# A mixture-of-experts stack: the four experts with the fewest tokens on raw float32 weights in two column halves, and expert weights in 8 KB rows

## The chip, the cores and the metric

The kernel runs on one core of one Trainium2 chip. The metric is the device time of one execution, in microseconds (us). Times that are compared come from repeated runs; the profile is one execution, taken by the hardware profiler. TensorE multiplies, VectorE (DVE) and ScalarE (ACT) do elementwise work, POOL is GpSimd, and SP issues the weight transfers.

## The reference, cut to what matters

An input of 256 tokens with 1024 features goes through two stacks of two layers. Layers of the first stack hold two kinds of attention and a feed-forward network; layers of the second hold a dilated attention beside an mLSTM. The first layer of the second stack has a dense feed-forward network, the second one eight experts, of which every token uses two:

```python
def swiglu(x, w13, w2):
    a, g = jnp.split(x @ w13, 2, axis=-1)
    return (jax.nn.silu(a) * g) @ w2

def moe_ffn(x, router_w, router_b, w13, w2):
    logits = (x @ router_w).astype(jnp.float32) + router_b.astype(jnp.float32)
    top_v, top_i = lax.top_k(logits, TOP_K)
    wts = jax.nn.softmax(top_v, axis=-1)
    gate = jnp.einsum('bsk,bske->bse', wts, jax.nn.one_hot(top_i, N_EXPERTS, dtype=jnp.float32)).astype(x.dtype)
    y = jnp.zeros_like(x)
    for e in range(N_EXPERTS):
        y = y + gate[..., e:e + 1] * swiglu(x, w13[e], w2[e])
    return y
```

An expert has a hidden width of 3584, so its three matrices are 11.01 million float32 numbers, 44.04 MB. With the inputs of the reference the router gives the experts 52, 36, 120, 63, 64, 53, 51 and 73 tokens.

## The kernel before

**Weights.** All weights stream from memory once, in the order of their use, in pieces of 1 MB (`Weights.add`, `Stream.load`, issued by SP at L200). Each piece goes to the next slot of a cycle (`_CYCLES`). For the experts the cycle has fourteen slots: four parts of the `wide` tile, four groups of four small tiles `s2` (four transfers of 256 KB each, 2 KB in a partition's row), four `raw` tiles, one pair of `bc` tiles (two transfers of 512 KB), and the tile `xTl`. A slot is loaded again as soon as its piece is used (`self.done`).

**Three passes.** `Stream.ahead` splits a piece, two blocks of 128 x 512 at a time: ScalarE copies it to `wh` in a shorter float format (L218), VectorE takes `wl` = raw - `wh` (L219). The input is split in the same way, and `mac` (L363) makes three matmuls of a block:

```python
        nc.tensor.matmul(out, xh, wh, start=first, stop=False)
        nc.tensor.matmul(out, xh, wl, start=False, stop=False)
        nc.tensor.matmul(out, xl, wh, start=False, stop=last)
```

They are L366, L367 and L368 in the rows. `wh` and `wl` have five tiles each, of two blocks.

**An expert** (`expert`, L1384) has room for 128 tokens. `gather` (L1351) picks its tokens by a one-hot matmul (L1366) and transposes them; 14 hidden blocks of 256 units take 8 weight blocks each, and after every 6, 4 and 4 of them (`_SEG`) the second matrix takes 4 blocks per hidden block: 168 blocks in 42 pieces. `hidden` multiplies the two halves and transposes the result by two matmuls; `scatter` puts the rows back (L1409, L1410). Experts go in the order 0 to 7. The gather of the next expert begins in the last segment. An expert with more than 128 tokens would send the kernel through a second pass over all of them, under `tc.If`.

**The order of the rest.** Nothing is scheduled by the compiler. Work beside the matmuls is written as generators; `tick`, called after every two weight blocks, advances each of them by one step, and `_WAIT` says how many ticks a generator lets pass at a named point (`wait("s2")`), so that its input is ready when its next TensorE instruction comes up. `softmax_quad` (L628) does four score matrices of an attention: after `wait("s2")` it transposes the probabilities (L665), after `wait("s3")` it multiplies them with the values (L673). `head_norm` (L591) normalises queries and keys, with VectorE's L602 after a reciprocal root on POOL (L443, L444), four ticks later. In `first_block` (L806) the projections run in the order: queries, keys, first attention, values and the rest. In `second_block` (L1146): the gate z of the mLSTM, its input, queries, keys, values, the attention beside the mLSTM, the branch gates (VectorE adds, ScalarE takes tanh), then `branches` with the mLSTM's branch M ahead of the attention's A.

## Time and profile before

| What | Value |
|---|---|
| Time, median of 3 runs | 2345.89 us (2345.5 to 2346.64) |
| The profiled execution | 2344.98 us, its span 2343.2 us |
| TensorE matmuls | 2269.1 us busy, 97% |
| VectorE | 1822.2 us busy, 78% |
| ScalarE | 1441.0 us busy, 61% |
| Weights by SP's queue | 566.44 MB, 66.5% of 16 DMA engines |
| Transfers of expert weights | 217 of 1 MB, 384 of 256 KB, 44 of 512 KB |

A busy share is a mean over the span, and the span has two kinds of stretch: the two stacks with their attention, up to some 1340 us, and the experts, from there to 2326 us. The 40 slices in the profile show them side by side: one digit is the busy share of a slice of 58.6 us in tenths. Matmuls overlap on TensorE, so one matmul's bar is longer than the beat at which they follow each other; the beat is read from the starts. One float32 matmul leaves two records in the trace. An instruction's bracket names how long its engine had been idle before it and whose work ended that.

### The profile page before, as it was taken

How to read it: one execution, taken by the hardware profiler on the slowest of the kernel's cores; microseconds unless marked ns; L12 is line 12 of the kernel's file. 1: busy time of each engine (PE TensorE's matmuls, PEld its weight loads, DVE VectorE, ACT ScalarE, POOL GpSimd, SP SyncE). 2: the span in 40 equal slices, each digit the busy share in tenths (PEclk: the TensorE clock that was granted, in tenths of full speed). 3: DMA queues.
4: the chain of work that ended last, by engine and by line, in shares of the span. 5: the costliest groups of instructions: out<-in, count | busy, mean ns of one | idle time of the engine just before them, and what ended most of it. 6: DMA issues, size and time to landing. Idle time of an engine off the chain costs nothing. (4 is left out here: it accounts for less than half of the span.)

```text
span 2343.2 us, 30976 instructions
## 1 busy us (share of the span) xinstructions
PE 2269.1 (97%) x11041; PEld 1859.9 (79%) x11041; DVE 1822.2 (78%) x2672; ACT 1441.0 (61%) x2166; POOL 100.3 (4%) x163
## 2 busy tenths in 40 slices
PE   6999999999999999999998899999999999999997
PEld 5778888778888977788886688888888888888775
DVE  5866556867565677655767799999999999999988
ACT  4555444555444554444454488888888888888775
POOL 4100001100010000000100000000000000000000
PEclk9999999999999999999999899999999999999998
DMA  6435555435565444554544799999999999999981
GB/s 238 159 138 180 182 186 204 167 126 180 180 233 205 154 136 168 197 198 164 184 168 141 300 362 371 354 370 349 371 349 370 349 373 341 376 339 376 332 334 47
DMA packets 128162, 583.06 MB, mean 249 GB/s; under 512 B 14592, under 2 KB 14880, under 8 KB 74624
## 3 DMA queue, kind: packets, MB, share of 16 engines
q1 hardware_dynamic: 124416, 566.44, 66.5%
q0 software_dynamic: 3584, 14.56, 1.9%
q8 instruction: 89, 1.46, 0.2%
q14 instruction: 73, 0.60, 0.1%
HBM read 579.90 MB, written 1.05 MB: 248 GB/s over the span
## 5 line engine op out<-in xcount | busy, mean ns | idle before, releaser
L219 DVE TENSOR_TENSOR wl<-raw,wh 128x1024 fp32r<-128x1024 f32 x594 | 711.7, 1229 | 147.8 <-ACT wh L218 145.1
L366 PE MATMUL mm<-wh,xTh 128*128 128x512 f32 (+1 forms) x1904 | 762.0, 400 | 6.7 <-DVE s L602 3.3
L367 PE MATMUL mm<-wl,xTh 128*128 128x512 f32 (+1 forms) x1904 | 742.5, 390 | 8.8 <-DVE wl L219 8.8
L218 ACT CAST wh<-raw 128x1024 fp32r<-128x1024 f32 x594 | 611.9, 1050 | 122.6 <-PE mm L368 110.0
L366 PEld LDWEIGHTS mm<-wh,xTh 128*128 128x128 f32 x1904 | 359.3, 189 | 82.6 <-issue 11.7
L367 PEld LDWEIGHTS mm<-wl,xTh 128*128 128x128 f32 x1904 | 359.8, 189 | 76.0 <-DVE wl L219 9.9
L368 PE MATMUL mm<-wh,xTl 128*128 128x512 f32 (+1 forms) x1008 | 392.4, 389 | 2.1 <-DVE xTl L455 1.9
L366 PE MATMUL mm<-wh,s 128*128 128x512 f32 x968 | 386.2, 399 | 0.0
L368 PE MATMUL mm<-wh,s 128*128 128x512 f32 x968 | 378.5, 391 | 0.2 <-DVE s L458 0.2
L367 PE MATMUL mm<-wl,s 128*128 128x512 f32 x968 | 378.0, 391 | 0.0
L368 PE MATMUL mm<-wh,xTh 128*128 128x512 f32 x896 | 349.7, 390 | 0.0
L219 DVE TENSOR_TENSOR wl<-s,wh 128x512 fp32r<-128x512 f32 x384 | 242.2, 690 | 14.1 <-ACT wh L218 10.8
L219 DVE TENSOR_TENSOR wl<-wide,wh 128x1024 fp32r<-128x1024 f32 x196 | 235.1, 1222 | 17.0 <-ACT wh L218 6.2
L218 ACT CAST wh<-s 128x512 fp32r<-128x512 f32 x384 | 217.4, 620 | 23.2 <-PE mm L368 21.7
L218 ACT CAST wh<-wide 128x1024 fp32r<-128x1024 f32 x196 | 204.1, 1055 | 36.4 <-PE mm L368 33.0
L368 PEld LDWEIGHTS mm<-wh,xTl 128*128 128x128 f32 x1008 | 190.9, 189 | 43.7 <-DVE xTl L455 4.3
L366 PEld LDWEIGHTS mm<-wh,s 128*128 128x128 f32 x968 | 182.5, 189 | 39.4 <-issue 2.5
L368 PEld LDWEIGHTS mm<-wh,s 128*128 128x128 f32 x968 | 182.1, 188 | 39.7 <-DVE s L458 0.8
L367 PEld LDWEIGHTS mm<-wl,s 128*128 128x128 f32 x968 | 182.6, 189 | 35.3
L368 PEld LDWEIGHTS mm<-wh,xTh 128*128 128x128 f32 x896 | 168.3, 188 | 36.0
L454 ACT CAST s<-ax 128x256 fp32r<-128x256 f32 x178 | 66.4, 373 | 163.5 <-PE ax L452 163.5
L455 DVE TENSOR_TENSOR s<-ax,s 128x256 fp32r<-128x256 f32 x178 | 75.1, 422 | 68.2 <-ACT s L454 68.2
(287 smaller groups left out, 1934.0 us busy)
## 6 DMA issues: line engine op xcount, KB each, us to landing
raw<-in_wpre SPq DMA_DIRECT2D x197, 1024.0 KB, 4.8
wide<-in_wexp SPq DMA_DIRECT2D x97, 1024.0 KB, 6.5
s<-in_wexp SPq DMA_DIRECT2D x384, 256.0 KB, 6.4
raw<-in_wexp SPq DMA_DIRECT2D x96, 1024.0 KB, 6.6
xTl<-in_wexp SPq DMA_DIRECT2D x24, 1024.0 KB, 6.9
bc<-in_wexp SPq DMA_DIRECT2D x44, 512.0 KB, 6.9
raw<-in_wpre SPq DMA_DIRECT2D x8, 512.0 KB, 3.5
wide<-in_bias_b POOLq DMA_DIRECT2D x2, 1536.0 KB, 9.6
```

The source lines that it names most:

```text
L218: nc.scalar.copy(h, raw)
L219: nc.vector.tensor_tensor(l, raw, h.bitcast(F32), op=ALU.subtract)
L366: nc.tensor.matmul(out, xh, wh, start=first, stop=False)
L367: nc.tensor.matmul(out, xh, wl, start=False, stop=False)
L368: nc.tensor.matmul(out, xl, wh, start=False, stop=last)
L454: nc.scalar.copy(hi, ps)
L455: nc.vector.tensor_tensor(lo, ps, hi.bitcast(F32), op=ALU.subtract)
```

## The change

There are three edits.

1. **Ranking.** The experts are worked in order of their token counts, the large and the small ones alternating (`_RANK`): places 0, 2, 4 and 6 take the four with the most tokens, places 1, 3, 5 and 7 the four with the fewest; expert 0 always stands first. `rest`, the tail of the router, computes the ranks, and SP reads the index of the expert from the tile `r_which` (`place`, a register load) for the address of each piece. The small places have room for 64 tokens, and the second pass runs if an expert has more than its room.
2. **Raw weights.** In the small places no weight is split. The moving operand is the raw float32 block where the transfer put it; the stationary one is the input, 128 x 64 float32. Even blocks write the partitions 0 to 63 of the result, odd ones 64 to 127 (`tile_position`), so that two blocks use the two halves of the array's columns. `hidden_few` adds the halves and transposes at once, by four float32 matmuls with the 128 x 64 constant `fold2`. A slot becomes free when its matmuls are issued (`gone`), not when it is split.
3. **Slots.** The cycle of the expert weights has nine slots, all of 1 MB with 8 KB in a partition's row: `wide` four times, `raw` four times, `xTl`.

With them come moves in the blocks ahead: the first layer of `first_block` projects the values before the queries, `head_norm` waits five ticks instead of four, `second_block` takes the values first and z after the attention has begun, its gates are generators of their own, and branch A comes ahead of M. The waits s2 and s3 go from 4 and 3 to 5 and 4, and stay at 4 and 3 (`s2x`, `s3x`) in the attention beside the mLSTM; `h2` is 2. The table `_WAIT` and the constants' declarations are left out here.

```diff
+_RANK = [0, 4, 1, 5, 2, 6, 3, 7]
+_SMALL = 64
+_ROOMS = [_SMALL if r > 3 else 128 for r in _RANK]
...
-_FIRST, _THEN = ["0", "1", "2", "3", "s2a"], ["raw"] * _BUFS["raw"] + ["bc", "xT"]
-_CYCLES = [_FIRST + ["s2b", "s2c", "s2d"] + _THEN]
...
+_CYCLES = [["0", "1", "2", "3"] + ["raw"] * _BUFS["raw"] + ["xT"]]
...
-    ("bias", 3072, 1), ("v129", 2064, 1), ("m_g", 512, 1), ("junk", 256, 1), ("early", 800, 1),
+    ("bias", 3072, 1), ("v129", 2064, 1), ("m_g", 512, 1), ("junk", 256, 1), ("early", 928, 1),
...
-        if a == "bc":
-            return [k.row(1024).rearrange("p (n w) -> p n w", w=w) for _ in range(2)], 1024 // w
...
-        if a[:2] == "s2":
-            return [k.s2(1, 512) for _ in range(n)], 1
...
-            if self.held and self.slots[self.loaded][0] in ("bc", "xT"):
+            if self.held and self.slots[self.loaded][0] == "xT":
...
-                e = self.e if e < 0 else e
+                e = self.e if e < 0 else k.place(e)
...
-            p, j, m = parts[self.split]
+            p, j, m, plain = parts[self.split]
...
+            if plain:
+                self.ready[self.split] = [tiles[(j + i) // per][:, (j + i) % per] for i in range(m)]
+                self.split += 1
+                continue
...
-                del self.raw[p]
-                self.done = p
-                self.load(0)
+                self.gone(p)
...
+    def gone(self, p):
...
+        del self.raw[p]
+        self.free.add(p)
+        while self.done + 1 in self.free:
+            self.done += 1
+        self.load(0)
...
+        p, _, _, plain = self.order.parts[self.over]
...
+        if plain and (self.over == len(self.order.parts) or self.order.parts[self.over][0] != p):
+            self.gone(p)
...
-        for _ in range(4):
+        for _ in range(5):
...
-        yield from self.wait("s2")
+        yield from self.wait("s2" if beside is None else "s2x")
...
-            self.evac(p, pt)
+            nc.scalar.copy(p, pt)
...
-        yield from self.wait("s3")
+        yield from self.wait("s3" if beside is None else "s3x")
...
+                    self.finish(*self.late)
...
-        self.project(xT, 8, W(0, 512), later(prep_q), outer=4)
-        if not self.dry:
+        values = lambda outer: self.project(xT, 8, W(1792, 512), keep_v, outer=outer)
+        if l == 0:
+            values(4)
+        if not self.dry and l == 0:
...
+        self.project(xT, 8, W(0, 512), later(prep_q), outer=4 if l else 0)
...
-        self.project(xT, 8, W(1792, 512), keep_v)
+        if l:
+            values(0)
...
-        self.project(xT, 8, [("w_in_2", (l,), 2048, 512)], tanh_z, outer=4)
+        def keep_v(t, ps):
+            va[t] = self.s2(512)
+            self.evac(va[t], ps)
...
+        qT, kT, va = {}, {}, {}
+        self.project(xT, 8, [("w_in_2", (l,), 1024, 512)], keep_v, outer=4)
...
-        qT, kT, va = {}, {}, {}
...
-        def keep_v(t, ps):
-            va[t] = self.s2(512)
-            self.evac(va[t], ps)
...
-        self.project(xT, 8, [("w_in_2", (l,), 1024, 512)], keep_v)
...
+        self.project(xT, 8, [("w_in_2", (l,), 2048, 512)], tanh_z)
...
-                def gate(t, ps):
-                    g = G[t][:, D * n + 512 * j : D * n + 512 * j + 512]
-                    V.tensor_tensor(g, ps, bg[:, 512 * j : 512 * j + 512], op=ALU.add)
+                def gate(t, ps, g, b):
+                    V.tensor_tensor(g, ps, b, op=ALU.add)
+                    yield
...
-                self.project(xT, 8, [("w_gate_2", (l,), D * n + 512 * j, 512)], gate)
...
+                at = D * n + 512 * j
+                self.project(
+                    xT, 8, [("w_gate_2", (l,), at, 512)],
+                    lambda t, ps: gates.append(self.go(gate(t, ps, G[t][:, at : at + 512], bg[:, 512 * j : 512 * j + 512]))),
+                )
...
-        self.branches(G, ((M, ym, "w_br_m_2", 1), (A, ya, "w_br_a_2", 0)), l)
+        self.late = gates
+        self.branches(G, ((A, ya, "w_br_a_2", 0), (M, ym, "w_br_m_2", 1)), l)
...
-            V.reduce_max(most, ps, axis=AX.X)
...
+            n, rank, over, most, at = self.tiny(8), self.tiny(8), self.tiny(8), self.tiny(1), self.tiny(8)
+            every = [128, 8, 8]
+            V.tensor_tensor(n, ps, self.c("tie8"), op=ALU.add)
+            more, place = self.s2(8, 8), self.s2(8, 8)
+            V.tensor_tensor(more, n[:, None, :].to_broadcast(every), n[:, :, None].to_broadcast(every), op=ALU.is_gt)
+            V.reduce_sum(rank, more, axis=AX.X)
+            V.tensor_scalar(self.rooms, rank, 3.5, _SMALL - 128.0, op0=ALU.is_gt, op1=ALU.mult)
+            V.tensor_scalar(self.rooms, self.rooms, 128.0, None, op0=ALU.add)
+            V.tensor_tensor(over, ps, self.rooms, op=ALU.subtract)
+            V.reduce_max(most, over, axis=AX.X)
...
+            yield
...
+                place, rank[:, None, :].to_broadcast(every), self.c("rank8")[:, :, None].to_broadcast(every), op=ALU.is_equal
...
+            V.tensor_tensor(more, place, self.c("index8")[:, None, :].to_broadcast(every), op=ALU.mult)
+            V.reduce_sum(at, more, axis=AX.X)
+            V.tensor_copy(self.which, at)
+            yield
...
+                V.tensor_tensor(got, place[:, None].to_broadcast(both), src[:, :, None, :].to_broadcast(both), op=ALU.mult)
+                V.reduce_sum(dst, got, axis=AX.X)
+                yield
...
+    def place(self, i):
...
+        if i not in self.places:
+            self.places[i] = self.nc.values_load(
+                self.which[0:1, i : i + 1], engines=(mybir.EngineType.SP,), min_val=0, max_val=NE - 1
...
+        return self.places[i]
...
-            V.tensor_scalar(oh[:, t], self.c("iota"), key[:, t], None, op0=ALU.is_equal)
+            V.tensor_scalar(oh[:, t], self.c("iota" if room == 128 else "iota2"), key[:, t], None, op0=ALU.is_equal)
...
+        both = self.tl(self.keep, "xTh", [128, 2, 8, 128], F32R if room == 128 else F32)
...
-            self.split_T(lambda i: rows[n][:, 128 * i : 128 * i + 128], 4, both[:, 0, z], both[:, 1, z])
...
+            if room == 128:
+                self.split_T(src, 4, both[:, 0, z], both[:, 1, z])
+            else:
+                self.to_T(src, 4, both[:, 0, z, 0:room])
...
+        many = room == 128
...
+        def product(out, a, b, k, i, n):
...
+            if many:
+                self.mac(out, (a[:, 0, k], a[:, 1, k]), b, i == 0, i == n - 1)
...
+            z = 64 * (i % 2)
+            T.matmul(out[z : z + 64], a[:, 0, k, 0:room], b, start=i < 2, stop=i >= n - 2, tile_position=(0, z))
...
+        def hidden_few(j, ps):
+            u = self.s2(512)
+            nc.scalar.copy(u, ps)
+            yield from self.wait("h2")
+            ps = self.ax(4, room)
+            for i in range(4):
+                T.matmul(ps[:, i], u[:, 128 * i : 128 * i + 128], self.c("fold2"), start=True, stop=True)
+            u = self.s2(2, 2, room)
+            nc.scalar.activation(u[:, 0], ps[:, 0:2], AF.Silu)
+            V.tensor_tensor(u[:, 1], ps[:, 2:4], u[:, 0], op=ALU.mult)
+            hT[j] = u[:, 1:2]
...
-            self.split_T(lambda i: u[:, 1, 128 * i : 128 * i + 128], 2, d[:, 0:2], d[:, 2:4])
...
+            self.split_T(lambda i: u[:, 1, 128 * i : 128 * i + 128], 2, d[:, 0], d[:, 1])
...
-                        self.mac(ps, (xh[:, k], xl[:, k]), b, k == 0, k == 7)
+                        product(ps, xT, b, k, k, 8)
...
-                        gens[j] = self.go(hidden(j, ps))
+                        gens[j] = self.go((hidden if many else hidden_few)(j, ps))
...
-                        d = hT[k // 2]
-                        self.mac(y[n], (d[:, k % 2], d[:, 2 + k % 2]), b, k == 0, k == nk - 1)
+                        product(y[n], hT[k // 2], b, k % 2, k, nk)
...
-        n = nc.values_load(self.most[0:1, 0:1], min_val=0, max_val=S)
-        with tc.If(n > 128):
-            V.tensor_scalar(self.key, self.key, -128.0, None, op0=ALU.add)
+        n = nc.values_load(self.most[0:1, 0:1], min_val=0, max_val=2 * S)
+        with tc.If(n > 256):
+            V.tensor_tensor(self.key, self.key, self.rooms[:, None, :].to_broadcast([128, 2, 8]), op=ALU.subtract)
```

On TensorE, at the start of the second expert (`mm_12403` is its first hidden result, `xTh` its input, L1409 and L1410 are the scatter of the expert ahead), this was the order before:

```order
L366 MATMUL mm_12403<-wh_12346,xTh_12282 128x512
L367 MATMUL mm_12403<-wl_12347,xTh_12282 128x512
L368 MATMUL mm_12403<-wh_12346,xTh_12282 128x512
L1409 MATMUL ax_12425<-s_2517_12397,s_2189_11101 128x512
L1410 MATMUL ax_12425<-s_2518_12398,s_2189_11101 128x512
L366 MATMUL mm_12403<-wh_12361,xTh_12282 128x512
L367 MATMUL mm_12403<-wl_12362,xTh_12282 128x512
```

and this is it after; L1471 is the float32 matmul, L1501 and L1502 are the scatter of the expert ahead, L1479 is the fold:

```order
L1471 MATMUL mm_12250<-raw_11958,xTh_12151 64x512 x4
L1501 MATMUL ax_12255<-s_2456_12244,s_2177_11073 128x512
L1502 MATMUL ax_12255<-s_2457_12245,s_2177_11073 128x512
L1471 MATMUL mm_12250<-raw_11984,xTh_12151 64x512 x2
L1501 MATMUL ax_12263<-s_2456_12244,s_2177_11073 128x512
L1502 MATMUL ax_12263<-s_2457_12245,s_2177_11073 128x512
L1471 MATMUL mm_12250<-raw_11984,xTh_12151 64x512 x2
L1471 MATMUL mm_12273<-xTl_12019,xTh_12151 64x512 x2
L1479 MATMUL ax_12276<-cst_78,s_2464_12269 128x64 x4
```

A pair of blocks that had six matmuls has two, one for each half of the result's partitions, and the hidden block ends in four fold matmuls among them.

On SP, in a part of the first expert, the slots were filled like this before (`in_wexp` holds the expert weights):

```order
L200 DMA raw_10891<-in_wexp 128x2048
L200 DMA raw_10929<-in_wexp 128x2048
L200 DMA bc_11104<-in_wexp 128x1024
L200 DMA bc_11105<-in_wexp 128x1024
L200 DMA xTl_11108<-in_wexp 128x2048
L200 DMA wide_74<-in_wexp 128x2048 x4
L200 DMA s_2226_11236<-in_wexp 128x512
L200 DMA s_2227_11237<-in_wexp 128x512
```

and after, up to the first piece of the second expert:

```order
L203 DMA xTl_11779<-in_wexp 128x2048
L203 DMA wide_74<-in_wexp 128x2048 x4
L203 DMA raw_11900<-in_wexp 128x2048
L203 DMA raw_11926<-in_wexp 128x2048
L1411 TENSOR_LOAD r_which_11069
L1411 ISA x2
L203 ISA
L203 DMA raw_11958<-in_wexp 128x2048
L203 ISA
L203 DMA raw_11984<-in_wexp 128x2048
```

The transfers of 128 x 512 and 128 x 1024 are gone, and each piece of a ranked expert stands behind an instruction that computes its address; the register load from `r_which` stands once ahead of an expert.

On TensorE, in the first layer of the second stack, at the end of its attention, before (L452 are transposes of the mLSTM, L665 those of the last four score matrices):

```order
L366 MATMUL mm_7336<-wh_7323,xTh_6043 128x512
L367 MATMUL mm_7336<-wl_7324,xTh_6043 128x512
L368 MATMUL mm_7336<-wh_7323,xTl_6044 128x512
L452 MATMUL ax_7458<-cst_78,s_1440_7272 128x128 x4
L665 MATMUL ax_7465<-cst_78,s_1464_7400 128x128 x4
L665 MATMUL ax_7471<-cst_78,s_1465_7401 128x128 x4
L366 MATMUL mm_7455<-wh_7355,s_1446_7306 128x512
```

and after, the transposes of the last four score matrices (now L684), and further on those of the mLSTM (now L471):

```order
L387 MATMUL mm_7375<-wh_7250,xTl_6044 128x512
L684 MATMUL ax_7399<-cst_78,s_1440_7279 128x128 x4
L684 MATMUL ax_7405<-cst_78,s_1441_7280 128x128 x4
L385 MATMUL mm_7382<-wh_7250,xTh_6043 128x512
L386 MATMUL mm_7382<-wl_7251,xTh_6043 128x512
L387 MATMUL mm_7382<-wh_7250,xTl_6044 128x512
```

```order
L385 MATMUL mm_7485<-wh_7389,s_1407_7110 128x512
L386 MATMUL mm_7485<-wl_7390,s_1407_7110 128x512
L387 MATMUL mm_7485<-wh_7389,s_1408_7111 128x512
L471 MATMUL ax_7494<-cst_78,s_1450_7318 128x128 x4
L385 MATMUL mm_7478<-wh_7417,s_1333_6776 128x512
```

The two groups of transposes, which stood next to each other, stand apart, with matmuls of the gates and of branch A between them.

## Rows read from the trace of the kernel before

**Rows 1.** The page's 40 slices of the whole span: matmuls, TensorE's granted clock, DMA, rate.
```profile
PE   6999999999999999999998899999999999999997
...
PEclk9999999999999999999999899999999999999998
DMA  6435555435565444554544799999999999999981
GB/s 238 159 138 180 182 186 204 167 126 180 180 233 205 154 136 168 197 198 164 184 168 141 300 362 371 354 370 349 371 349 370 349 373 341 376 339 376 332 334 47
```

**Rows 2.** Windows: stretch, its length, busy us (instructions) by engine, clock, DMA share, GB/s.
```profile
1400.00:1800.00 400.00, 400.00 (x1816) 328.57 (x1815) 376.72 (x478) 327.07 (x461) 0.00 (x0) 1.00 0.97 361
```

**Rows 3.** Timeline of TensorE at experts' start, inside, end: start us, us, engine, line, operation.
```profile
1340.71 0.54 PE L366 MATMUL mm<-wh,xTh 128*128 128x512 f32 x1
...
1379.84 0.39 PE L366 MATMUL mm<-wh,s 128*128 128x512 f32 x1
...
1380.52 0.39 PE L366 MATMUL mm<-wh,s 128*128 128x512 f32 x1
...
2326.09 0.39 PE L368 MATMUL mm<-wh,s 128*128 128x512 f32 x1
```

**Rows 4.** The gather line L1366 in two stretches: count, durations ns, first and last start.
```profile
L1366 PE MATMUL ax<-gate,s x8: 389/389/389, 1434.8 to 1437.8; 128*128 128x512 f32 x8
...
L1366 PE MATMUL ax<-gate,s x8: 389/389/398, 2172.2 to 2175.2; 128*128 128x512 f32 x8
```

**Rows 5.** Windows of the experts chosen by what the DMA moves in them.
```profile
1290.00:1300.00 10.00, 10.00 (x53) 8.32 (x52) 9.42 (x12) 4.62 (x6) 0.00 (x0) 1.00 1.01 423
1300.00:1310.00 10.00, 10.00 (x46) 8.27 (x45) 7.25 (x9) 5.65 (x6) 0.00 (x0) 1.00 1.00 334
1410.00:1417.00 7.00, 7.00 (x34) 5.73 (x33) 6.70 (x8) 5.60 (x7) 0.00 (x0) 1.00 1.01 417
1490.00:1497.00 7.00, 7.00 (x34) 5.74 (x33) 6.45 (x9) 5.99 (x8) 0.00 (x0) 1.00 1.01 403
1503.00:1510.00 7.00, 7.00 (x33) 5.79 (x32) 6.47 (x7) 5.48 (x7) 0.00 (x0) 1.00 1.00 362
```

**Rows 6.** Timeline of TensorE: float32 matmuls in column groups and their neighbours, both blocks.
```profile
84.83 1.09 PE L673 MATMUL ax<-s,s 128*64 128x128 f32 x14 [1.50 <-DVE s L433]
...
794.85 1.03 PE L990 MATMUL ax<-s,s 128*128 128x256 f32 x4
...
797.03 0.28 PE L419 MATMUL mm<-xTh,wl 128*128 128x256 f32 x1
797.24 1.50 PE L998 MATMUL ax<-s,s 128*32 128x256 f32 x24
...
798.89 0.28 PE L418 MATMUL mm<-xTl,wh 128*128 128x256 f32 x1
```

**Rows 7.** Waits of TensorE: waiting line, awaited line: us in total, times, longest us.
```profile
PE ax L665 <- DVE s L658: 9.3, 2, 4.7
PE mm L367 <- DVE wl L219: 8.8, 2, 8.3
...
PE ax L673 <- DVE s L433: 4.9, 4, 1.5
PE ax L673 <- ACT s L431: 3.5, 4, 1.5
```

**Rows 8.** Timeline of POOL, VectorE and TensorE around 37 us; idle before and releaser in brackets.
```profile
35.14 1.68 POOL L444 TENSOR_TENSOR tiny<-tiny,mhalf 128x8 f32<-128x8 f32 x1
...
36.86 0.75 DVE L602 SCALAR_TENSOR_TENSOR s<-mm,rms,tiny 128x512 f32<-128x512 f32 x1 [12.68 <-POOL tiny L444]
...
39.38 0.58 PE L367 MATMUL mm<-wl,xTh 128*128 128x256 f32 x1 [8.29 <-DVE wl L219]
```

**Rows 9.** Windows of the 20 us ahead of the first expert's matmuls.
```profile
1320.00:1330.00 10.00, 5.18 (x25) 3.54 (x24) 9.49 (x15) 5.22 (x7) 0.99 (x1) 0.69 0.69 255
1330.00:1340.00 10.00, 6.12 (x25) 4.78 (x24) 6.17 (x19) 1.28 (x3) 0.00 (x0) 0.67 0.80 303
```

More of the change, by code (lines that the diff above doesn't have):

```diff
@@ L65, in _constants @@
     early["upper"] = (p[:, None] <= p[None, :]).astype(float)
-    cols["supper"] = (p[:, None] < p[None, :]).astype(float)
+    early["supper"] = (p[:, None] < p[None, :]).astype(float)
     cols["ones"] = np.ones((128, 128))
@@ L70, in _constants @@
     cols["rev8"] = np.tile((8.0 - np.arange(8))[None, :], (128, 1))
+    cols["iota2"] = np.tile(p[None, :] % _SMALL + 1.0, (128, 1))
+    cols["fold2"] = (p[:, None] % _SMALL == np.arange(_SMALL)[None, :]).astype(float)
+    cols["index8"] = np.tile(np.arange(8.0)[None, :], (128, 1))
+    cols["tie8"] = np.tile(np.where(np.arange(8) == 0, 1000.0, -np.arange(8) / 16.0)[None, :], (128, 1))
+    cols["rank8"] = np.tile(np.array(_RANK, float)[None, :], (128, 1))
     got = []
@@ L125, in __init__, with add @@
         self.size = {}
-    def add(self, blocks, w, e):
+    def add(self, blocks, w, e, raw):
         name = "wpre" if e is None else "wexp"
@@ L147, in __init__ @@
         self.raw, self.ready = {}, {}
-        self.done, self.held, self.lead = -1, True, _AHEAD
+        self.done, self.held, self.lead, self.free = -1, True, _AHEAD, set()
         self.slots, last, used = [], {}, {}
@@ L160, in __init__ @@
             a = ring.pop(0)
-            if a == "bc" and i >= len(order.pieces) - 28:
-                a = ring.pop(0)
             used[a] = used.get(a, -1) + 1
@@ L280, in __init__ @@
         self.ticks, self.begun, self.quads = 0, -100, 0
+        self.late = []
+        self.places = {0: 0}
     def tl(self, pool, tag, shape, dt=F32):
@@ L345, in finish, with begin @@
                 self.tick()
-    def begin(self, blocks, w=512, e=None):
+    def begin(self, blocks, w=512, e=None, raw=False):
         if self.dry:
-            self.order.add(blocks, w, e)
+            self.order.add(blocks, w, e, raw)
     def parts(self, n, w=512):
@@ L626, in scores, with softmax_quad @@
         return ps
-    def softmax_quad(self, t, h0, q, k, v, bias, nk, sink, hi, lo):
+    def softmax_quad(self, t, h0, q, k, v, bias, nk, sink, hi, lo, beside):
         nc = self.nc
@@ L706, in attention @@
                     out[t] = self.s2(4, 128, dt=F32R), self.s2(4, 128, dt=F32R)
-                gen = self.softmax_quad(t, h0, q, k, v, bias, nk(t), sink, *out[t])
+                gen = self.softmax_quad(t, h0, q, k, v, bias, nk(t), sink, *out[t], beside)
                 next(gen)
@@ L1325, in route @@
         self.most = self.tl(self.small, "r_most", [128, 1], I32)
+        self.which = self.tl(self.small, "r_which", [128, 8], I32)
+        self.rooms = self.tl(self.small, "r_rooms", [128, 8])
+        self.gates, self.keys = keep("r_gates"), keep("r_keys")
         def rest():
@@ L1381, in gather, with expert @@
         nc.scalar.copy(oh[:, 2:4], ps)
-        got += [oh, both[:, 0], both[:, 1]]
-    def expert(self, e, got, gate, between, added):
+        got += [oh, both]
+    def expert(self, e, got, gate, between, added, room=128):
         nc = self.nc
@@ L1423, in expert @@
             for j in range(done, done + seg):
-                self.begin([(128 * k, [("exp_w13_2", (0,), 256 * j, 256), ("exp_w13_2", (0,), FE + 256 * j, 256)]) for k in range(8)], e=e)
+                self.begin([(128 * k, [("exp_w13_2", (0,), 256 * j, 256), ("exp_w13_2", (0,), FE + 256 * j, 256)]) for k in range(8)], e=e, raw=not many)
                 ps = self.mm(512)
@@ L1435, in expert @@
             for n in range(2):
-                self.begin([(128 * k, [("exp_w2_2", (0,), 512 * n, 512)]) for k in range(2 * done, 2 * (done + seg))], e=e)
+                self.begin([(128 * k, [("exp_w2_2", (0,), 512 * n, 512)]) for k in range(2 * done, 2 * (done + seg))], e=e, raw=not many)
                 for k0, blocks in self.parts(2 * seg):
@@ L1458, in gather @@
             got = []
-            return self.go(self.gather(col(self.key, e), got)), got
+            if e:
+                self.finish(rest)
+            return self.go(self.gather(col(self.keys if e else self.key, e), got, _ROOMS[e])), got
         self.free = True
```

28 lines of the change are left out of this document (18 added, 10 removed).

## The prediction

> **What bounds the kernel now.** I read the page's slices first. In 40 slices the matmul row of TensorE stands at 9 in all but the first and three others, at a granted clock of 9 tenths or more in all but two [rows 1]. From the 24th slice on run the eight experts: there the DMA row stands at 9 too, down to the last two, and moves 332 to 376 GB/s. So in the experts two resources are full at once, and I had to learn which one ends last. The window of 400 us in the middle of the experts says it: TensorE is busy 400.00 of 400.00 us at a clock of 1.00, the DMA engines 0.97, VectorE 376.72 [rows 2]. TensorE sets the time; the DMA follows 3% behind, and it will be the next bound.
>
> The timeline gives the beat: three matmuls of 512 columns take 0.68 us (1379.84 to 1380.52), 0.2267 us each [rows 3]. The gather line L1366 starts at 1434.8 for one expert and at 2172.2 six experts later [rows 4]: 737.4 / 6 = 122.9 us for an expert. It has 42 pieces of 4 blocks, three passes each, 504 matmuls: 504 x 0.2267 = 114.3 us. The other 8.6 are transposes, gather and scatter. Eight experts are 983 us, which agrees with the first expert matmul at 1340.71 and the last at 2326.09 [rows 3].
>
> **Part 1, the matmuls of the four small experts.** Removed: 504 fp32r matmuls per small expert. Added: per pair of blocks two float32 matmuls of 64 output columns, one in each half of the array, 84 pairs. Only the rows of the attention show float32 and column groups. A matmul's bar outlasts its beat by 0.16 us: 0.39 against 0.2267 for 512 columns [rows 3]. Taken off the end of each group, the lone float32 group at 794.85, 4 records of 256 columns in 1.03, has (1.03 - 0.16) / 4 = 0.217 a record, and the L998 group, 24 records in four column groups or six rounds in 1.50, (1.50 - 0.16) / 6 = 0.223 a round [rows 6]. So four groups run side by side in the time of one (one behind the other, 24 records would want over 5 us). A round of 512 columns is 0.45, a float32 matmul makes two records, and a pair of blocks costs 0.90, against 6 x 0.2267 = 1.36 now. The lower end is the lone record's pace, 0.87. The upper end charges everything around L998 to its rounds: from L419 at 797.03 to L418 at 798.89 it is 1.86, less two matmuls of 256 columns at 0.12 (half of 0.2267, and a little) = 1.62, / 6 = 0.27 [rows 6], thus 1.08 a pair. I take 0.90, the row of the column groups themselves: 84 x 0.90 = 75.6 us.
>
> Each of 14 hidden blocks leaves column mode for four float32 fold matmuls, 8 records. L673 has seven rounds of 128 columns in 1.09 us [rows 6], (1.09 - 0.16) / 7 = 0.133 each; the fold's 64 columns may take half of that, I take all. Going out of column mode and back is what is left of the 1.62 above: 1.62 - 6 x 0.223 = 0.28. That is 14 x (8 x 0.133 + 0.28) = 18.8 us, at half a record 11.4. Gather and scatter stay: the 8.6 less 28 transposes of 0.133 = 4.9, plus some nine more switches, 2.5. A small expert: 75.6 + 18.8 + 7.4 = 101.8 us on TensorE instead of 122.9. What it gives back to VectorE and ScalarE, which split no weights there, is off the path, since both lie beside the matmuls already [rows 2].
>
> The Trainium skill ("TensorE: Matmul & The Clock Gate", Part 3, Measured speedup vs the span model) has three column tiles at 2.38 times one, not 3. By that a pair would cost 0.90 x 3 / 2.38 = 1.13, a small expert 121.5 us, and the time would be about 2320; the rows of L998 speak for less, four groups at 0.223 against a lone record's 0.217.
>
> **Part 2, the DMA.** Bytes stay: 44.04 MB an expert. Gone are the 256 KB and 512 KB pieces; nine slots of 1 MB replace fourteen. Windows where almost only 1 MB pieces travel move 423, 417, 403 and 362 GB/s, the one with 256 KB pieces 334 [rows 5]. The four average 401; I take 390, since a window of 7 us chosen for its pieces misses the gaps. A pair of experts, one big, one small, then needs 88.08 MB / 390 = 226 us of DMA against 122.9 + 101.8 = 224.7 of TensorE. That is close to a tie. The order big, small, big, small lets the nine waiting pieces (9.4 MB) carry what the big expert leaves over (122.9 x 390 = 47.9 MB, 3.9 more than it eats) into the small one. In a tie neither hides the other wholly, so 227 per pair, four pairs 908, against 983: **-75 us**. Bounds: 220 per pair with the DMA at 401, 0.87 a pair of blocks and the cheap fold (-103); 243 at 362 GB/s (-10). The edit of SP's issue order, one register read and a computed address ahead of every piece, costs nothing: SP issues 42 pieces and 42 addresses where it issued 81 pieces, and stays ahead by nine pieces. The register waits for the ranking, which is done early in the first expert, while SP wants it only when the second expert's first piece has a free slot; if it were late, one such wait would drain the nine pieces (25 us of cover).
>
> **Part 3, the ranking.** Some 15 small VectorE instructions join the router's tail. None has a row; the 0.75 us of the 512-column L602 [rows 8] is an upper end, 11 us in all, nothing the lower one. They have at most 128 elements a row and come bit by bit beside the first expert, with split weights waiting: 0.
>
> **Part 4, the two blocks ahead.** Four waits of TensorE are aimed at [rows 7]. The 8.3 us of L367 on the split L219: POOL's L444 ends late (35.14 plus 1.68), VectorE's L602 has idled 12.68 us for it, the split stands behind L602, and TensorE waits until 39.38 [rows 8]. With the values projected ahead of the queries no norm stands ahead of the next splits, and the norm's wait is a tick longer: -8. What is late next is the queries' own norm, with the keys' matmuls before it. The two waits of 4.7 at L665, transposes of the last softmax: 18 matmuls stand between its scores and its transposes, and 42 after the change; the 24 more are 24 x 0.2267 = 5.4 us, more than 4.7: -9. The mLSTM's transposes, until now just ahead of them, move behind 18 + 24 matmuls and find their input done. The L673 waits, 4.9 and 3.5 in all, lose part to the one tick more: -3. Together **-20**, bounds 0 (each wait goes to the next late operand) and -29 (all four rows and the clock after them).
>
> **The sum.** -75 - 20 = -95, against the profiled execution's 2344.98 (2343.2 of it span): 2250. The median of the runs lies 0.9 above the profiled run, which I let go in the rounding.
>
> **Rivals.** (A) **The DMA does not get faster.** The 1 MB pieces move at the slowest of my windows, 362 GB/s [rows 5]: 243 a pair, 973 in all, -10 and -20: 2315. For it: the page's slices never pass 376 over 59 us [rows 1]. Against: the slices hold 256 KB pieces in 4 of 14 slots, and TensorE was the bound there. The Trainium skill ("DMA: Bandwidth & Descriptors", Where 436 GB/s comes from) says the memory side binds at about 358 for a core; by that a pair is 246 and the time 2326. The window at 423 over 10 us [rows 5] speaks against it here. Chance 0.17.
>
> (B) **The halves share badly.** 1.08 per pair of blocks, everything that L998's surroundings can be charged with: 84 x 1.08 + 26.2 = 116.9, a pair of experts 239.8, in all 959: -24 - 20, 2301. It is against the even pace of the L998 group. Chance 0.08.
>
> (C) **Slower: column halves run one after the other, or at half the clock.** In the 20 us ahead of the experts TensorE was busy 5.18 and 6.12 of 10 us and was granted 0.69 and 0.67 [rows 9], between the levels of 1.2 and 2.4 GHz. If the small experts, waiting for weights and leaving column mode 14 times, fell to the lower level, or if two halves ran as four rounds, a pair of blocks costs 1.80 and a small expert 151.2 + 26.2 = 177.4: (122.9 + 177.4) x 4 = 1201, +218 - 20, 2543. It loses from 1.21 us per pair of blocks on ((122.9 + 5 - 26.2) / 84, the 5 being a quarter of the 20). Against it: L998 [rows 6], and a TensorE that has 101.8 us of work in the 104 (227 - 122.9) it gets. Chance 0.06.
>
> (D) **The change does not do what it says:** an expert that has more tokens than its 64 rooms sends the kernel through the pass for overflow, all experts again, some 1000 us more. The reference's router gives the four small ones 63, 53, 51 and 36 tokens; 63 fits. Chance 0.01. (E) Only the bytes count, the blocks ahead give nothing, and the time stays within 0.2%: 0.02.
>
> **How the numbers follow.** Forecast 0.66 (2212 to 2280), A 0.17 (2285 to 2326), B 0.08, C 0.06, D 0.01, E 0.02. A measurement of this kernel tells 0.2% from no change, some 4.7 us. Forecast, A and B are faster: 0.91. E and the edge of A are the same: 0.02 and 0.01, 0.03. C and D, with little rounding: 0.06. The low end is nearly all bounds at their best, -103 - 29 = 2213, taken as 2215. The high end is 2305, past B and into A: the upper part of A, with C, D and E, is left out, about 0.2.
>
> **What would show it.** In the profile after: gather starts of every second expert about 227 us apart; in a small expert the f32 line with groups of 64 output partitions, 0.90 per pair; the DMA at 385 to 395 GB/s through the experts with a share of 1.00; the waits of L367 and L665 gone from the table of waits. A pair of 243 at a full DMA share makes A right, a small expert with TensorE always busy and over 110 us makes B right, and a granted clock under 0.95 there is C.

## The result and the profile after

The changed kernel takes 2217.62 us (median, 2214.89 to 2219.23) against 2345.69 for the kernel before in the same comparison: a ratio of 0.9454, 95% interval 0.9438 to 0.9471, 128 us less. The forecast was 95 less, 2250, with a range of 2215 to 2305. The profiled execution took 2214.89 us, its span 2213.1.

These are the page's slices of the changed kernel, now 55.3 us each: matmuls, VectorE, the granted clock, the DMA and its rate. They answer to [rows 1].

```profile
PE   6999999999999999999999989999999999999997
DVE  5766556777656568855567889804980498049812
PEclk9999999999999999999999999999999999999999
DMA  7434555544555644655554649899999999999996
GB/s 275 161 134 167 178 190 188 183 143 154 189 202 204 210 140 160 204 186 191 182 188 153 219 184 383 336 389 419 419 369 393 420 419 363 398 420 418 359 386 261
```

VectorE's digits show the experts in turn: 9 and 8 while it splits for a large one, 0 in the middle of a small one. TensorE stays at 9, so in both kinds of expert it is still the engine that is full, and the DMA row is at 9 beside it. The DMA's rate now reaches 420 GB/s in single slices, where [rows 1] never passed 376.

Windows over whole experts, in turn small and large (stretch, length, busy us and instructions of TensorE, its weight loads, VectorE, ScalarE and POOL, clock, DMA share, GB/s), answer to [rows 2]:

```profile
1437.00:1533.00 96.00, 96.00 (x475) 39.27 (x474) 10.94 (x25) 17.27 (x35) 0.00 (x0) 1.00 0.97 395
1533.00:1658.00 125.00, 123.40 (x560) 100.78 (x558) 113.69 (x124) 95.59 (x117) 0.00 (x0) 1.00 0.99 403
1658.00:1754.00 96.00, 96.00 (x475) 39.28 (x474) 11.34 (x25) 17.67 (x36) 0.00 (x0) 1.00 0.97 396
1754.00:1878.00 124.00, 122.85 (x559) 100.75 (x558) 113.30 (x123) 95.23 (x116) 0.00 (x0) 1.00 0.99 405
1974.00:2100.00 126.00, 124.01 (x557) 101.28 (x554) 114.23 (x123) 96.44 (x117) 1.99 (x4) 0.99 0.99 401
```

A small expert is 96.0 us with TensorE busy all the time; it never waits for weights there. A large one is 124 to 126 with 1.2 to 2.0 us of idle TensorE. The timeline of TensorE gives the ends of the stretches and the inside of a small expert (start us, us, engine, line, operation); it answers to [rows 3]:

```profile
1312.55 0.50 PE L385 MATMUL mm<-wh,xTh 128*128 128x512 f32 x1
...
1437.02 1.51 PE L1471 MATMUL mm<-raw,xTh 128*64 128x512 f32 x6
...
1448.75 3.65 PE L1471 MATMUL mm<-wide,xTh 128*64 128x512 f32 x16
1452.33 1.10 PE L1479 MATMUL ax<-cst,s 128*128 128x64 f32 x8
1453.37 1.08 PE L1471 MATMUL mm<-wide,xTh 128*64 128x512 f32 x4
...
2197.23 1.08 PE L1471 MATMUL mm<-wide,s 128*64 128x512 f32 x4
```

The first expert matmul comes at 1312.55 instead of 1340.71, 28.2 us earlier. From there to the last pair of blocks at 2197.72 (the second pair's half of the last row) are 885.2 us instead of 985.4, 100.2 less. The tail behind it is 1.7 shorter. 28.2 + 100.2 + 1.7 = 130.1, the difference of the two profiled executions (2344.98 - 2214.89).

Inside a small expert, 16 records, four pairs of blocks, take 1452.33 - 1448.75 = 3.58 us, and a fold takes 1453.37 - 1452.33 = 1.04 us. Both hold some of the change between column mode and the full array. The beat without it is read from records further inside; the same stretch, with its rows cut at other places:

```profile
1449.66 2.75 PE L1471 MATMUL mm<-wide,xTh 128*64 128x512 f32 x12
1451.80 0.60 PE L1471 MATMUL mm<-wide,xTh 128*64 128x512 f32 x2
1452.33 0.43 PE L1479 MATMUL ax<-cst,s 128*128 128x64 f32 x2
```

From 1449.66 to 1451.80 are ten records, two and a half pairs of blocks: 2.14 / 2.5 = 0.857 us a pair. Two records of the fold are 0.43 long and all eight 1.10, so one record takes 0.67 / 6 = 0.112. From fold to fold are 3.58 + 1.04 = 4.62 us; four pairs and eight records make 3.43 + 0.90 of it, and 0.29 are left for going out of column mode and back. In a small expert that is 84 x 0.857 + 112 x 0.112 + 14 x 0.29 = 72.0 + 12.5 + 4.1 = 88.6, and 7.4 are left for gather and scatter.

The waits of TensorE (us in total, times, longest) answer to [rows 7]:

```profile
PE mm L385 <- DVE s L621: 8.4, 3, 3.3
...
PE ax L1502 <- DVE s L1497: 5.0, 4, 2.0
...
PE ax L684 <- DVE s L677: 1.6, 1, 1.6
```

L684 and L677 are the old L665 and L658. Both waits of 4.7 us in the second stack are gone; the 1.6 us are another wait, in the first stack. The 8.3 us of L367 on the split are gone too, and a norm that is late (L621, the old L602, 3.3 before) took part of their place. New is L1502, the scatter of a small expert, which stands where VectorE begins to split for the large one behind it. VectorE's timeline there, and the matmul that waits:

```profile
1536.05 1.21 DVE L226 TENSOR_TENSOR wl<-raw,wh 128x1024 fp32r<-128x1024 f32 x1
1537.18 0.68 DVE L1497 TENSOR_TENSOR s<-mm,s 128x512 fp32r<-128x512 f32 x1
1537.78 2.35 DVE L226 TENSOR_TENSOR wl<-raw,wh 128x1024 fp32r<-128x1024 f32 x2
```

```profile
1537.92 0.50 PE L1502 MATMUL ax<-s,s 128*128 128x512 f32 x1 [1.60 <-DVE s L1497]
```

L1497, which the scatter needs, waits its turn on VectorE behind a split of 1.21 us.

### The profile page after: what moved, and what is told of

Read it like the earlier page. It is cut to its first block, busy times and chain, and to the rows that moved or that the text cites. A ratio compares the mean times of both kernels' runs of the same rounds, so it can differ in the third digit from the quotient of the medians.

```text
span 2213.1 us, 28515 instructions
## 1 busy us (share of the span) xinstructions
PE 2157.1 (97%) x10705; PEld 1612.3 (73%) x10705; DVE 1385.1 (63%) x2075; ACT 1101.0 (50%) x1658; POOL 104.5 (5%) x163
## 5 line engine op out<-in xcount | busy, mean ns | idle before, releaser
L385 PE MATMUL mm<-wh,xTh 128*128 128x512 f32 (+1 forms) x1456 | 584.4, 401 | 11.4 <-DVE s L621 8.4
L386 PE MATMUL mm<-wl,xTh 128*128 128x512 f32 (+1 forms) x1456 | 567.6, 390 | 0.5 <-DVE wl L226 0.5
L385 PEld LDWEIGHTS mm<-wh,xTh 128*128 128x128 f32 x1456 | 275.1, 189 | 72.1 <-issue 16.9
L386 PEld LDWEIGHTS mm<-wl,xTh 128*128 128x128 f32 x1456 | 275.8, 189 | 52.0 <-DVE wl L226 1.4
L385 PE MATMUL mm<-wh,s 128*128 128x512 f32 x744 | 296.4, 398 | 0.0
L387 PE MATMUL mm<-wh,s 128*128 128x512 f32 x744 | 290.6, 391 | 0.0
L386 PE MATMUL mm<-wl,s 128*128 128x512 f32 x744 | 290.0, 390 | 0.0
L226 DVE TENSOR_TENSOR wl<-wide,wh 128x1024 fp32r<-128x1024 f32 x152 | 181.4, 1222 | 16.7 <-ACT wh L225 11.0
L387 PE MATMUL mm<-wh,xTh 128*128 128x512 f32 x448 | 175.8, 392 | 0.7 <-DVE xTh L474 0.7
L387 PEld LDWEIGHTS mm<-wh,s 128*128 128x128 f32 x744 | 139.6, 188 | 30.1
L385 PEld LDWEIGHTS mm<-wh,s 128*128 128x128 f32 x744 | 139.7, 188 | 28.1 <-issue 1.0
L387 PEld LDWEIGHTS mm<-wh,xTh 128*128 128x128 f32 x448 | 84.4, 188 | 19.8 <-DVE xTh L474 1.5
L1471 PE MATMUL mm<-raw,xTh 128*64 128x512 f32 x408 | 96.5, 600 | 0.0
```

Source lines behind the costliest of these rows:

```text
L226: nc.vector.tensor_tensor(l, raw, h.bitcast(F32), op=ALU.subtract)
L1471: T.matmul(out[z : z + 64], a[:, 0, k, 0:room], b, start=i < 2, stop=i >= n - 2, tile_position=(0, z))
```

## The experiments

All ten are compared with the kernel before on the same chip; a change is told against the changed kernel's 2217.6.

**Faster transfers without small experts.**

```diff
-_ROOMS = [_SMALL if r > 3 else 128 for r in _RANK]
+_ROOMS = [128 for r in _RANK]
```

> The changed kernel with 128 rooms in all eight places: every expert takes the three passes of split weights, none the raw float32; nine slots of 1 MB, the ranking and the moves in the blocks stay. Theory 1 (TensorE was the bound, at 122.9 us for an expert, and faster transfers alone give nothing): the experts take 983 us as before, only the blocks' gain of some 28 us is left, 2316 us, the DMA share well under 0.95. Theory 2 (before, the 256 KB transfers held the kernel back now and then): under 2300. The time of the changed kernel for comparison: 2217.6.

Measured: 2318.20 us, ratio 0.9881 (0.9865 to 0.9898). Theory 1. From the first expert matmul to the last are 985.6 us (1314.95 to 2300.55), as in the kernel before (985.4): without the small experts the new slots give nothing, and no cost of the ranking shows. What remains, 27 us, is the blocks' gain. The window in the middle of its experts (columns as above):

```profile
1400.00:1800.00 400.00, 400.00 (x1822) 329.53 (x1821) 373.63 (x403) 320.63 (x386) 0.00 (x0) 1.00 0.94 360
```

The DMA moves 360 GB/s at a share of 0.94, all in 8 KB rows that can move 420 at a share of 1.01 (below). The share fell far less than the room there is, 60 of 420 GB/s; why is not shown. The 0.97 of [rows 2] was therefore no sign that only 3% of the DMA were left.

**Small experts with the transfers of before.**

```diff
+                if name == "wexp":
+                    step = {4: 1, 5: 1, 6: 1, 7: 1, 12: 2}.get(self.loaded % 14, step)
```

> The changed kernel with small experts on raw weights, but of every 14 pieces four are fetched as four transfers of 256 KB (2 KB in a row) and one as two of 512 KB, as before; nine slots stay. Theory 1 (the small experts use up what the 8 KB rows give): before, 361 GB/s at a DMA share of 0.97, so about 372 at a full share; a pair of experts 88.08 / 372 = 237 us against 220.6, +65 us, 2283 us, with TensorE waiting for transfers inside the small experts. Theory 2 (short rows cost nothing as long as nine slots are ahead): 2218.

Measured: 2240.41 us, ratio 0.9546 (0.9530 to 0.9562), 23 us slower than with 1 MB transfers only. Neither number came: the smaller transfers cost something, about a third of what theory 1 gave.

**All expert weights in short rows.**

```diff
+                if name == "wexp":
+                    step = 1
```

> The changed kernel with every piece of the experts fetched as four transfers of 256 KB, 2 KB in a row; nine slots, raw small experts and the moves in the blocks stay. It asks what a short row costs by itself, since the run with 5 of 14 pieces in smaller transfers lost 23 us where 65 were expected. Theory 1 (a 2 KB row moves at the 334 to 350 GB/s of the windows before the change): 88.08 / 345 = 255 us a pair of experts against 220.6, +139 us, 2357 us. Theory 2 (the windows before were slow because the slots came free late, not because the rows are short; rows cost a few per cent): 395 to 405 GB/s, 220 to 223 a pair, 2218 to 2235.

Measured: 2277.45 us, ratio 0.9711 (0.9695 to 0.9727), +60 us, between the theories. In its windows over a large expert, and over a small one, the DMA is the bound, with the share above 1:

```profile
1545.00:1670.00 125.00, 122.25 (x555) 99.74 (x555) 113.48 (x123) 95.87 (x118) 0.00 (x0) 1.00 1.04 374
1670.00:1776.00 106.00, 104.74 (x452) 41.09 (x448) 7.80 (x21) 14.05 (x32) 0.00 (x0) 1.00 1.02 363
```

Its pairs of experts take 235, 241 and 238 us (first small matmul to the next large expert's end), 88.08 MB / 238 = 370 GB/s. So a stream of 256 KB transfers with 2 KB rows moves 370 GB/s here, and the window at 334 in [rows 5] was a bad guide. With five of fourteen pieces short, the bytes would want (9/14) / 420 + (5/14) / 370, 401 GB/s, 220 us a pair, just what TensorE needs. The other run's pairs take 224 to 230. There a stretch of short pieces falls well below 370; why is not shown:

```profile
1902.00:1908.00 6.00, 6.00 (x36) 2.97 (x32) 0.29 (x1) 1.15 (x3) 0.00 (x0) 1.00 0.95 273
```

This run makes the rows short and the transfers small at once. The issues from 1900 to 2000 us (KB each, median us from issue to landing), here and, below, in the run with the small experts in a row:

```profile
raw<-in_wexp SPq DMA_DIRECT2D x60, 256.0 KB, 5.6
raw<-in_wexp SPq DMA_DIRECT2D x19, 1024.0 KB, 19.1
```

At 370 and 420 GB/s that is about 2 MB under way at any time here and 8 MB there. Counted from issue and landing, no run has more than eight transfers of expert weights under way at once. In the changed kernel, in stretches of 1 us with only two 1 MB transfers under way, the DMA moves 369 GB/s too, with four or more 420. But in the run of old rows, in the 24 us in which 2 KB rows run with 3.2 to 4.5 MB under way, they also move 369. Whether the length of the rows or the little that is under way sets the 370 is open.

**The order of the experts.**

```diff
-_RANK = [0, 4, 1, 5, 2, 6, 3, 7]
+_RANK = [0, 1, 2, 3, 4, 5, 6, 7]
```

> The changed kernel with the four large experts first and the four small ones last, instead of in turn. Theory 1 (a small expert at 96 us wants 459 GB/s, the DMA gives some 405, and what waits in nine slots bridges one small expert only): four small ones need 4 x 108.7 less the 23 us of the slots, 412 against 384, +28 us, 2245 us, with TensorE waiting inside the last three. Theory 2 (the DMA has room to spare and share 0.97 is only the refilling of free slots): 2218.

Measured: 2231.82 us, ratio 0.9515 (0.9500 to 0.9531), 14 us slower, between the theories. The four small ones take 409.8 us, 412 were expected; the large ones lie at 122.6 each, without the waits at L1502, and pay nearly half of it back. In the run of small experts the DMA is the bound and shows what it can do, and TensorE waits for it:

```profile
1830.00:1898.00 68.00, 68.00 (x338) 27.78 (x336) 5.63 (x16) 9.67 (x22) 0.00 (x0) 1.00 1.01 419
1900.00:2000.00 100.00, 93.85 (x452) 36.38 (x448) 7.63 (x21) 13.61 (x31) 0.00 (x0) 1.00 1.01 420
```

```profile
PE mm L1471 <- DMA wide<-in_wexp: 6.0, 12, 0.7
PE mm L1471 <- DMA raw<-in_wexp: 5.2, 10, 0.7
```

**Raw float32 without column halves.** Its sums are doubled by the repeated tokens and halved again. The main lines of the edit:

```diff
-            z = 64 * (i % 2)
-            T.matmul(out[z : z + 64], a[:, 0, k, 0:room], b, start=i < 2, stop=i >= n - 2, tile_position=(0, z))
+            T.matmul(out, a[:, 0, k], b, start=i == 0, stop=i == n - 1)
```

> The changed kernel without column halves: in the small experts every block is one float32 matmul with 128 columns (the 64 tokens twice), the doubled sums are halved in the fold and in the scatter; same bytes, same number of matmuls. Theory 1 (two halves run at the same time): a pair of blocks takes four rounds of 0.43 instead of two, 84 x 0.86 = 72 us more in each small expert, +289 us, 2507 us, slower than before the change. Theory 2 (the halves run one behind the other already, and the small experts gain only from being float32 without a split): 2218.

Measured: 2470.78 us, ratio 1.0528 (1.0507 to 1.0549). Theory 1, with 253 us for 289. The same sixteen records, one fold before them and one behind:

```profile
1456.09 1.05 PE L1478 MATMUL ax<-cst,s 128*128 128x128 f32 x8
1456.98 7.03 PE L1470 MATMUL mm<-wide,xTh 128*128 128x512 f32 x16
1463.85 0.38 PE L1478 MATMUL ax<-cst,s 128*128 128x128 f32 x2
```

1463.85 - 1456.98 = 6.87 us for sixteen records, 0.859 a matmul of two: a block alone takes as long here as a pair of blocks in two halves (0.857). So the two halves of the array run wholly at the same time, by a factor of 2.00; with the changes of mode, 6.87 against 3.58, it is 1.92. The fold takes 1456.98 - 1456.09 = 0.89, 0.111 a record of 128 columns, where one of 64 columns took 0.112. A small expert is 161.1 us here, 7 less than the 96 + 72 expected: no column mode has to be left. With 0.29 for each of 14 folds and of the nine more switches that the prediction counts, that is 6.7. Raw float32 alone loses to the three passes; the halves turn it.

**Half of the small experts' matmuls.** Every second pair of blocks is left out of the sums; the weights are all fetched.

```diff
-            T.matmul(out[z : z + 64], a[:, 0, k, 0:room], b, start=i < 2, stop=i >= n - 2, tile_position=(0, z))
+            if i // 2 % 2 == 0:
+                T.matmul(out[z : z + 64], a[:, 0, k, 0:room], b, start=i < 2, stop=i >= n - 4, tile_position=(0, z))
```

> The changed kernel with every second pair of blocks left out of the matmuls of the small experts (their sums lack half of the terms); all weights are still fetched. TensorE would need 96 - 36 = 60 us for a small expert. Theory 1 (the DMA stands just behind TensorE, some 405 GB/s): a pair of experts 217.5 us instead of 220.6, 2205 us, with TensorE waiting for transfers. Theory 2 (the DMA has room): down to 2218 - 4 x 36 = 2074.

Measured: 2200.90 us, ratio 0.9376 (0.9357 to 0.9395). Theory 1: with 36 us less to do in each small expert, 17 us are gained in all. A small expert still takes 91 us, and TensorE waits for transfers 63 us in all:

```profile
1440.00:1530.00 90.00, 73.93 (x306) 29.60 (x302) 8.64 (x22) 14.32 (x33) 0.00 (x0) 0.85 0.99 407
```

```profile
PE mm L1472 <- DMA wide<-in_wexp: 29.3, 34, 1.5
PE mm L1472 <- DMA raw<-in_wexp: 24.8, 32, 1.6
PE mm L1472 <- DMA xTl<-in_wexp: 8.8, 8, 1.5
```

A TensorE that waits so often was granted 0.85 of its clock in the mean of this window, between the levels of 1.2 and 2.4 GHz; in the changed kernel's small experts it had 1.00.

**Five small experts.**

```diff
-_RANK = [0, 4, 1, 5, 2, 6, 3, 7]
+_RANK = [0, 3, 1, 4, 5, 2, 6, 7]
...
-_ROOMS = [_SMALL if r > 3 else 128 for r in _RANK]
+_ROOMS = [_SMALL if r > 2 else 128 for r in _RANK]
...
-            V.tensor_scalar(self.rooms, rank, 3.5, _SMALL - 128.0, op0=ALU.is_gt, op1=ALU.mult)
+            V.tensor_scalar(self.rooms, rank, 2.5, _SMALL - 128.0, op0=ALU.is_gt, op1=ALU.mult)
```

> Five small places instead of four (the experts with 64, 63, 53, 51 and 36 tokens), in the order large, small, large, small, small, large, small, small. TensorE would need 27 us less (122.9 - 96). Theory 1 (the DMA at some 405 GB/s is next, 352.3 MB in 870 us against 885): -15 us, 2203 us. Theory 2 (TensorE alone decides): -27 us, 2191.

Measured: 2202.40 us, ratio 0.9383 (0.9367 to 0.9399), 15 us faster than the changed kernel and the fastest here that computes all. Theory 1's number. Two small experts in a row take 200.7 us instead of 192; in the second the DMA sets the time:

```profile
1680.00:1760.00 80.00, 80.00 (x394) 32.38 (x395) 8.84 (x21) 11.39 (x26) 0.00 (x0) 1.00 1.01 420
1760.00:1860.00 100.00, 94.28 (x458) 36.84 (x454) 8.37 (x22) 16.07 (x34) 0.00 (x0) 1.00 1.01 420
```

It rests on these inputs: the expert with 64 tokens just fits its 64 rooms.

**The blocks ahead, undone in three cuts.** First all the moves, for the two stacks, the waits and the copies (their main lines):

```diff
-        if l == 0:
-            values(4)
...
-            nc.scalar.copy(p, pt)
+            self.evac(p, pt)
...
-        self.project(xT, 8, [("w_in_2", (l,), 1024, 512)], keep_v, outer=4)
+        self.project(xT, 8, [("w_in_2", (l,), 2048, 512)], tanh_z, outer=4)
```

> The changed kernel with the edits in the two stacks ahead of the experts undone (values first, waits of five ticks, PSUM copies by ScalarE, z and the gates late, branch A ahead of M); the experts as changed. Theory 1: the first expert's matmul starts 28 us later, 2246 us, the experts take their 885 us as before. Theory 2 (part of the 28 comes from the slots or constants, not from these moves): under 2240.

Measured: 2248.83 us, ratio 0.9587 (0.9571 to 0.9603), +31. Theory 1: its first expert matmul starts as late as before, and its small experts take 96.0 us each, but for the last, 98.

Then the second stack alone:

```diff
-        self.project(xT, 8, [("w_in_2", (l,), 1024, 512)], keep_v, outer=4)
+        self.project(xT, 8, [("w_in_2", (l,), 2048, 512)], tanh_z, outer=4)
...
-        self.branches(G, ((A, ya, "w_br_a_2", 0), (M, ym, "w_br_m_2", 1)), l)
+        self.branches(G, ((M, ym, "w_br_m_2", 1), (A, ya, "w_br_a_2", 0)), l)
```

> The changed kernel with only the moves in the second stack undone (z first and values last, gates added and squashed at once, branch M ahead of A); the first stack, the waits and the experts as changed. Theory 1 (the trace has the second stack's two layers 10.5 and 10.9 us shorter, from the waits at the last softmax and the clock after them): 2217.6 + 21 = 2239. Theory 2 (the longer waits s2 and s3 and the copies on ScalarE are what counts): 2218 to 2225.

Measured: 2238.09 us, ratio 0.9542 (0.9526 to 0.9557), +20.5. Theory 1. The wait at the last softmax is back in its table of waits:

```profile
PE ax L684 <- DVE s L677: 11.0, 3, 4.7
```

And the first stack with the waits and copies alone:

```diff
-        if l == 0:
-            values(4)
...
+        self.project(xT, 8, W(0, 512), later(prep_q), outer=4)
...
-        for _ in range(5):
+        for _ in range(4):
```

> The changed kernel with the moves in the first stack, the waits s2, s3 and of the norm, and the copies by ScalarE undone; the second stack's order and the experts as changed. Theory 1 (the two stacks' moves add up; undoing both cost 31 us and undoing the second alone 20.5): 2217.6 + 10.7 = 2228. Theory 2 (either alone takes most of it, since the same last operand is late): 2240 or more.

Measured: 2231.23 us, ratio 0.9505 (0.9489 to 0.9521), +13.6. Theory 1 to 3 us: 20.5 + 13.6 = 34 against 31 for both.

These sums are good to some 3 us: in the eight runs that keep all the moves, the first expert matmul starts between 1310.25 and 1314.95.

## Why the prediction was right, and which terms were off

**What bounds the kernel** held: TensorE was the bound in the experts, and faster transfers alone gave nothing (the run with all experts large). The forecast had the DMA next, a little ahead of it; TensorE still sets the time.

**A pair of blocks** was forecast at 0.90 from the L998 group in [rows 6] and is 0.857, below the lower end of 0.87: the halves cost each other nothing. Rival B (halves that share badly, 1.08) is out. The Trainium skill ("TensorE: Matmul & The Clock Gate", Part 3, Measured speedup vs the span model) has three column tiles at 2.38 times one. Scaled to a pair, an estimate, that was 1.13; the trace does not agree with it, two halves of 64 give 2.00.

**The fold** was forecast at 8 x 0.133 + 0.28 and is 8 x 0.112 + 0.29. Going out of column mode and back was right. So was charging 64 columns like 128; the price of a record was too high. The pairs are 3.6 us cheaper than forecast and the folds 2.2; with the 7.4 for gather and scatter, which held, a small expert came to 96.0 instead of 101.8.

**The DMA** is the term that failed. I took 390 GB/s; where it is the bound, the runs show 420 over 100 us (the small experts in a row). The windows of 1 MB pieces in [rows 5] were taken from a kernel in which TensorE set the time, and I went below their average of 401. From there the near tie, 226 against 224.7, and the 227 that I made of it. TensorE sets the measured 221 (885.2 / 4). The experts' term is -100, not -75: 23 us from the cheaper small experts (4 x 5.8), 9 from charging the tie, 2 because the experts before took 985, not 983, and back some 9, because the large experts take 124 to 127 us instead of 122.9. Of these 9 the waits of L1502 are 5; I saw none of it, and that it cancels the charge for the tie is luck. The cheaper small experts count only because the DMA was faster too: at 390 GB/s the pair would have stayed at 226.

The wait of L1502 was of a kind the prediction should have named: the small experts give VectorE its rest, and at the seam the split for the next large expert is queued ahead of the scatter's own subtraction.

Yet the tie was not far away. 88.08 / 420 would be 210 us a pair, but with half of the matmuls gone two of the three pairs still take 218 and one 221, 404 GB/s at 218. In that run the DMA moves 420 in most of a large expert, and less when it nears its end (windows, columns as above):

```profile
1560.00:1600.00 40.00, 40.00 (x182) 32.95 (x181) 37.08 (x38) 32.53 (x38) 0.00 (x0) 1.00 1.01 420
1640.00:1657.00 17.00, 17.00 (x83) 14.07 (x82) 13.00 (x16) 9.80 (x14) 0.00 (x0) 1.00 0.89 343
```

In the 17 us of the second window SP waits for VectorE in 13, so the slots are full by then, and the small expert must fetch most of its own weights. That is why four small experts are nearly all that this stream can feed, and a fifth gave 15 us, not 27.

**Rival A** (362 GB/s) is out: 420 was held. The Trainium skill ("DMA: Bandwidth & Descriptors", Where 436 GB/s comes from) names 358 for the memory side; the trace does not agree. The same page of the Trainium skill (Bandwidth, Measured) has 425 GB/s for a transfer of 16 MB issued from GpSimd; the 420 here, issued by SP, lies near it. **Rival C** was priced too high: the run without column halves stands for halves one behind the other, and it lies at 2470.78, not 2543; that they would lose is shown. D and E did not come. **The ranking** was put at nothing, and the run with all experts large shows no cost of it.

**The blocks ahead** were forecast at -20 and gave -28.2. By the trace the first stack gave 6.3 (the start of the second stack moved from 765 to 759 us) for 8 forecast: L367's 8.3 us went, a late norm took some back. Undoing the first stack's moves cost 13.6; its trace begins the second stack 9.0 us later than the changed kernel, 2.7 later than the kernel before. Where these 2.7 come from is open. The second stack gave the other 21.9 for a forecast of 12. Its waits at L665 and L673 lost 14.6 us (9.3, and 5.3 of the 8.4) instead of 12; the rest, some 7 us, the forecast left out, and TensorE's clock behind a wait is a part of it. The timeline of the kernel before, after the 4.67 us of L665:

```profile
889.59 1.94 PE L665 MATMUL ax<-cst,s 128*128 128x128 f32 x8 [4.67 <-DVE s L658]
891.19 0.78 PE L366 MATMUL mm<-wh,s 128*128 128x512 f32 x1
891.76 0.63 PE L367 MATMUL mm<-wl,s 128*128 128x512 f32 x1
892.19 0.63 PE L368 MATMUL mm<-wh,s 128*128 128x512 f32 x1
892.61 0.63 PE L366 MATMUL mm<-wh,s 128*128 128x512 f32 x1
...
893.81 0.40 PE L366 MATMUL mm<-wh,s 128*128 128x512 f32 x1
```

```profile
888.00:896.00 8.00, 6.41 (x24) 5.45 (x25) 5.63 (x8) 4.00 (x8) 0.54 (x1) 0.64 0.35 112
```

The matmuls follow each other by 0.43 us, not 0.2267, and the window's clock is 0.64: the lower level, 1.2 GHz, for some of it. From 889.59 to 893.81 are 4.22 us for eight records of 0.112 and six matmuls of 0.2267, which make 2.26: about 2 us behind this wait, and a like wait stood in the other layer. What the remaining 3 us of the 7 are, no run separates. I had the clock in my upper bound of 29, not in the value.

**The sum.** Two terms erred in the same direction, 25 and 8 us, so the time landed near the low end of the range, 2215. The sign and the mechanism were right; the size was three quarters of what came.

## What to carry to other kernels

A part of a change can be worth nothing or less without another: larger transfers without cheaper experts gave nothing, and raw float32 without column halves lost 124 us to the kernel before. Cost them together, and ask which resource each one moves out of the way. Don't read a transfer rate, or a busy share of the DMA, out of a stretch that another engine sets: take a stretch in which the transfers are waited for. And where a wait such as the one of 4.67 us goes, count the clock behind it too.

## What was not expected of the hardware

The DMA held 420 GB/s for 100 us with 1 MB transfers in 8 KB rows, and some 370 with 256 KB transfers in 2 KB rows, of which no more than 2 MB were under way; which of the two it is, no run separates. Its share stood at 0.94 while it moved 360, and at 1.01 with 420, so the share hardly tells how much room is left. Two column halves of 64 ran float32 matmuls side by side at 2.00 times the pace of one, and going out of column mode and back cost 0.29 us. A fold record took the same with 64 columns as with 128.
